# Splits ahead of the first norm's squares and sums on VectorE; the last output tile in two token parts, each with its own norm and stores

## The chip, the core and the metric

The kernel runs on one core of a Trainium2 chip. Its engines work side by side, each through a list of its own in order: TensorE (PE; its weight loads are shown as PEld), VectorE (DVE), ScalarE (ACT), GpSimd (POOL) and SyncE (SP); SyncE and ScalarE also issue the transfers. The metric is device time in microseconds (us), as a median of runs.

## What is computed

One step of a hybrid decoder of two layers: a gated delta-rule mixer (layer 0) and an RWKV-7 mixer (layer 1), each followed by a causal convolutional FFN, for a prompt of 512 tokens with 16 meta tokens ahead of it, and for 8 sequences of 4 new tokens. Everything is float32. Cut to what matters here:

```python
def rmsnorm(x, g):
    y = x * lax.rsqrt(jnp.mean(x * x, axis=-1, keepdims=True) + 1e-6)
    return y * g

def conv_ffn(h, buf, w_up, conv_w, w_down):
    up2 = h @ w_up                               # 1024 -> 2 * 2816
    gt, up = up2[..., :D_FF], up2[..., D_FF:]
    gc, new_buf = causal_dwconv(buf, gt, conv_w) # three taps
    return (silu(gc) * up) @ w_down, new_buf     # 2816 -> 1024

for i in range(2):
    x = x + mixer_i(rmsnorm(x, norm_mix[i]), ...)
    x = x + conv_ffn(rmsnorm(x, norm_ffn[i]), ...)
y = rmsnorm(x, norm_final)
```

The outputs are y for 544 tokens and the mixers' and convolutions' new states.

## The kernel before

The activations lie transposed: eight tiles (m = 0 to 7) of 128 features by 560 tokens (528 of the prompt with the meta tokens, 32 of the samples); in the second FFN only the 544 tokens remain whose output is wanted. A matrix product is a sum of three products of TensorE: each float32 factor is split into hi (rounded to the type fp32r) and lo (the rest), and hi x hi, hi x lo and lo x hi are added up in PSUM (`dense_g`, line 115). A weight comes in pieces of up to eight tiles of 128 x 128: `load_piece` (lines 64 to 72) has ScalarE issue the transfer into raw, ScalarE makes hi, VectorE makes lo. raw, hi and lo have two buffers each, so a piece's hi has to wait until TensorE has used up the piece two before it. `E.plan` lists the pieces in their order; `fetch` loads one ahead.

A norm is not applied before the product that uses it. The squares of the eight x tiles are added up (class `Norm`, line 204: the first square into s, six more through sq, the eighth into sl), one-column matmuls with a column of ones sum them over the features (`sums`, line 231), VectorE works out the inverse root in eleven small instructions (`rsqrt`), matmuls spread it over the partitions (`spread`, line 244), and it is multiplied onto the product's result. x itself is only scaled by the norm's gain and split (`split_x`, lines 186 and 187: hi on ScalarE, lo on VectorE).

**The first inputs** (`first_input`). For each m: split, then `norm.add` with `spread=True`, so the squares alternate between ScalarE and VectorE; the six additions into s are GpSimd's (line 218). The first products are those of w_ab (32 columns) and of the first piece of w_in; both run over the eight x tiles as these become ready, and the norm's column sums follow them on TensorE.

**The last outputs** (`ffn` with layer 1, and the end of `body`). Each of the eight output tiles of the second FFN is a product over 22 tiles of h (pieces of 8, 8 and 6) in two halves of 272 tokens: 22 x 3 x 2 = 132 matmuls. VectorE adds the residual (xo, line 336), the sink squares it, adds the square and stores x times the gain in a tile that stays in SBUF (line 2022). After the eighth tile comes the final norm: sums, rsqrt, spread with two copies to SBUF (line 246), eight products y = x * s of 544 tokens (line 2053, two of them on GpSimd), and eight stores of 272 KB from a ring of three y tiles (line 2054).

The program is written as loops; a scheduler of the framework puts the instructions of each engine in order by a simulated timeline. So an edit at one place can also change the order elsewhere.

Of the kernel before, what the change touches and what calls it, by code (L numbers as in the profile page):

```python
# [8 lines left out]
F32 = mybir.dt.float32  # L9
# [3 lines left out]
ALU = mybir.AluOpType  # L13
# [47 lines left out]
    return E.pv[:, PV[name] + j:PV[name] + j + n]  # L61


def load_piece(E, src, kt, M, lo_eng, R=P):
    nc = E.nc
    raw = E.wp.tile([P, KD, P], F32, tag="raw", name="raw", bufs=2)
    hi = E.wp.tile([P, KD, P], F32R, tag="hi", name="hi")
    lo = E.wp.tile([P, KD, P], F32R, tag="lo", name="lo")
    nc.scalar.dma_start(out=raw[:R, :kt, :M], in_=src)
    nc.scalar.activation(hi[:R, :kt, :M], raw[:R, :kt, :M], AF.Copy)  # L70
    lo_eng.tensor_tensor(lo[:R, :kt, :M], raw[:R, :kt, :M], hi[:R, :kt, :M].bitcast(F32), op=ALU.subtract)  # L71
    return hi, lo
# [13 lines left out]
def plan(E, src, kts, M=P, eng=None, R=P):  # L86

    k = 0
    for kt in kts:
        E.plan.append((src[:, k:k + kt, :], kt, M, eng or E.nc.vector, R))  # L90
        k += kt
# [50 lines left out]
def dense(E, kts, xs, split, M=P, room=None, n=T):  # L142
    g = dense_g(E, kts, xs, split, M, None, room, n)
    while True:
        try:
            next(g)
        except StopIteration as e:
            return e.value
# [21 lines left out]
def big_pair(E, name, rings):  # L170

    return [big(E, F32R, name, r) for r in rings]


def tiles(pair, n=KD):
    return [(pair[0][:, k], pair[1][:, k]) for k in range(n)]
# [13 lines left out]
class Norm:  # L190
# [10 lines left out]
            self.E.nc.gpsimd.memset(t[:, self.w:], 1.0)  # L201
        return t

    def add(self, x, tmp, spread=False):
        E, nc = self.E, self.E.nc
        if self.n == 0:
            sq = self.acc
        elif self.n < KD - 1:
            sq = tmp.tile([P, T], F32, tag="sq", name="sq")
        else:  # L210
            sq = self.last = self.room("sl")
        sq = sq[:, :self.w]
        if spread and self.n % 2:
            nc.vector.tensor_tensor(sq, x, x, op=ALU.mult)
        else:
            nc.scalar.activation(sq, x, AF.Square)  # L216
        if 0 < self.n < KD - 1:
            nc.gpsimd.tensor_tensor(self.acc[:, :self.w], self.acc[:, :self.w], sq, op=ALU.add)  # L218
        self.n += 1

    def scale(self, bank):
# [25 lines left out]
        return self.acc  # L247


def first_input(E):  # L250

    nc = E.nc
    with ExitStack() as st:
        tp = E.pool("x0", 2, stack=st)
        norm, pair = Norm(E), big_pair(E, "x", (0, 0))
        xs = [tp.tile([P, T], F32, tag="x", name="x", bufs=KD) for _ in range(KD)]
        for m in range(KD):
            nc.sync.dma_start(out=xs[m], in_=E.I["xT"][m])
            if m == 3:
                nc.sync.dma_start(out=E.cm, in_=E.I["cm"])  # L260
        for m in range(KD):
            split_x(E, xs[m], pvec(E, "norm_mix0", m), pair[0][:, m], pair[1][:, m])
            norm.add(xs[m], tp, True)
    return pair, norm


def plan_ffn(E, layer):
    for j in range(KF):
        plan(E, E.I["w_up"][layer, j], [KD])
        plan(E, E.I["w_up"][layer, KF + j], [KD])  # L270
    for m in range(KD):
        plan(E, E.I["w_down"][layer, m], [8, 8, 6])


def ffn(E, layer, xs, norm, ring, x_dram, sink):

    nc, I, O = E.nc, E.I, E.O

# [7 lines left out]
    with ExitStack() as st:  # L286
# [3 lines left out]
        nc.sync.dma_start(out=state, in_=I["ffn_state"][layer])  # L290
        news = ar.tile([P, KF, 18], F32, tag="fnew", name="fnew")
        bank = bank_of(E.pool(f"ffnp{layer}", 3, PSUM, stack=st))
        hb = big_pair(E, "hb", ring)
        hs = []
        for j in range(KF):
# [36 lines left out]
        for m in range(KD):  # L332
            xo = tp.tile([P, n_main], F32, tag="xo", name="xo")
            nc.sync.dma_start(out=xo, in_=x_dram[m][:, :n_main])
            ps = dense(E, [8, 8, 6], hs, hw, n=n_main)
            nc.vector.tensor_tensor(two(xo), ps[:, :, :hw], two(xo), op=ALU.add)
            sink(m, xo, tp)
# [101 lines left out]
def bank_of(pg):  # L439
    def bank(shape):  # L440
        t = pg.tile([P, 512], F32, tag="pg", name="pg")
        n = int(np.prod(shape))
        v = t[:, :n]
        if len(shape) == 2:
            v = v.rearrange("p (a b) -> p a b", a=shape[0])
        elif len(shape) == 3:
            v = v.rearrange("p (a b c) -> p a b c", a=shape[0], b=shape[1])
        return v
    return bank
# [1548 lines left out]
def body(nc, tc, I, O):  # L1998
    with ExitStack() as st:
# [43 lines left out]
        gdn(E, p0, n0, I["xT"], then(big_pair, (0, 1), "norm_ffn0", res[0]))  # L2043
        ffn(E, 0, tiles(later["x"]), later["n"], (0, 1), res[0], then(big_pair, (0, 1), "norm_mix1", res[1]))
        rwkv(E, later["x"], later["n"], res[1], then(big_pair, (0, 0), "norm_ffn1", res[2]))
        ffn(E, 1, tiles(later["x"]), later["n"], (1, 1), res[2], then(big, 0, "norm_final", None))
        x = later["x"]
        s = later["n"].scale(bank_of(E.pool("pf", 3, PSUM)))
        tp = E.pool("fin", 3)
        for m in range(KD):  # L2050
            y = tp.tile([P, TL], F32, tag="y", name="y")
            eng = nc.gpsimd if m % 3 == 2 else nc.vector
            eng.tensor_tensor(y, x[:, m, :TL], s[:, :TL], op=ALU.mult)
            nc.sync.dma_start(out=O["y"][m], in_=y)


# [24 lines left out]
```

## Time and profile before

| | us |
|---|---|
| median of 3 runs | 1897.88 |
| fastest and slowest of them | 1892.95, 1904.3 |
| the profiled execution | 1895.85 |
| its span, from the first to the last instruction | 1894.0 |
| TensorE busy in the span | 1791.6 |
| VectorE, ScalarE, GpSimd busy | 1153.9, 731.3, 369.9 |
| mean granted clock of TensorE, as a share of full speed | 0.952 |

How to read the profile: times are us from the span's start. A row of the timeline has start, duration, engine, line, operation, out<-in, the count of merged instructions, and in brackets how long the engine had been idle and what ended that. In the chain of waits, a row has start, duration and what the end of the program was waiting for at that time. In the table of groups a row has busy time, mean ns of one, and the idle time before it with its releasers.

### The profile page before, as it was taken

The numbers are of one execution on the slowest core, as the hardware profiler recorded it, in microseconds if no ns is written. First come the engines' busy times: TensorE is split into PE (matmuls) and PEld (weight loads), VectorE is DVE, ScalarE is ACT, GpSimd is POOL, SyncE is SP. The second block draws the span as 40 slices with busy tenths as digits, with TensorE's granted clock in tenths as the row PEclk, the third lists the DMA queues.
The fourth block names the chain that finished last, engine by engine and source line by source line (L and its number), as shares of the span: only waits on it lengthen the run. The fifth ranks groups of instructions, "written<-read, shape, count | busy, mean of one in ns | idle before, by whom it ended". The sixth has DMA issues, their size and how long they took to land.

```text
span 1894.0 us, 36463 instructions
## 1 busy us (share of the span) xinstructions
PE 1791.6 (95%) x14675; PEld 1711.5 (90%) x14675; DVE 1153.9 (61%) x2321; ACT 731.3 (39%) x1479; POOL 369.9 (20%) x616
## 2 busy tenths in 40 slices
PE   7999999999999999998998999799997999999996
PEld 6889998789999999998788998688787999999996
DVE  6688973874555553336788986775666455554223
ACT  4776434442322232221882246444323222222221
POOL 3442402621222221114011010020001111111011
PEclk9999998999999999999897999797898899999998
DMA  4233232333222223434212244332255222222331
GB/s 132 77 88 99 65 97 100 145 117 131 83 85 90 81 88 100 122 118 120 72 63 67 83 115 127 93 97 84 76 152 156 86 88 90 90 90 91 101 109 67
DMA packets 128674, 186.23 MB, mean 98 GB/s; under 512 B 63753, under 2 KB 76041, under 8 KB 128505
## 3 DMA queue, kind: packets, MB, share of 16 engines
q10 hardware_dynamic: 34448, 111.63, 18.5%
q1 hardware_dynamic: 94056, 72.27, 13.2%
q8 instruction: 116, 1.90, 0.4%
q14 instruction: 54, 0.43, 0.1%
HBM read 151.63 MB, written 32.22 MB: 97 GB/s over the span
## 4 chain that ended last, share of the span: by engine, by line
PE 79%; DVE 10%; ACT 3%; DMA 2%; issue 1%; SPq 0%; POOL 0%; ACTq 0%; DVEq 0%
PE pd L115 58%; PE pd L138 3%; PE pg L1372 1%; PE pg L1674 1%; PE pg L1774 1%; PE pg L1651 1%; PE pg L1665 1%; PE pg L1647 1%; PE pg L1656 1%; DMA xo<-x 1%; DVE lo L71 1%; PE pg L835 1%; PE pg L627 1%; PE pg L1793 1%; PE pg L1466 0%
## 5 line engine op out<-in xcount | busy, mean ns | idle before, releaser
L115 PE MATMUL pd<-x,hi 128*128 128x280 f32 (+7 forms) x4768 | 838.1, 297 | 25.7 <-ACT hi L70 10.0
L115 PEld LDWEIGHTS pd<-x,hi 128*128 128x128 f32 (+1 forms) x4768 | 695.6, 192 | 33.1 <-ACT hi L70 10.2
L115 PE MATMUL pd<-x,lo 128*128 128x296 f32 (+5 forms) x2384 | 514.7, 297 | 5.9 <-DVE lo L71 5.9
L70 ACT ACTIVATE hi<-raw 128x1024 fp32r<-128x1024 f32 (+3 forms) x218 | 220.0, 1009 | 510.8 <-PE pd L115 476.6
L115 PEld LDWEIGHTS pd<-x,lo 128*128 128x128 f32 (+1 forms) x2384 | 383.5, 192 | 9.6 <-DVE lo L71 6.9
L71 DVE TENSOR_TENSOR lo<-raw,hi 128x1024 fp32r<-128x1024 f32 (+3 forms) x218 | 253.5, 1163 | 219.8 <-ACT hi L70 213.0
L218 POOL TENSOR_TENSOR s<-s,sq 128x560 f32<-128x560 f32 (+2 forms) x30 | 50.6, 1685 | 309.1 <-ACT sq L216 278.8
L304 DVE TENSOR_TENSOR gp<-pd,s 128x528 f32<-128x528 f32 (+1 forms) x44 | 30.8, 701 | 106.9 <-PE pd L115 106.8
L115 PE MATMUL pd<-hl,hi 128*128 128x280 f32 (+1 forms) x448 | 93.4, 290 | 0.0
L115 PE MATMUL pd<-hh,hi 128*128 128x280 f32 (+1 forms) x448 | 93.2, 289 | 0.0
L115 PE MATMUL pd<-hh,lo 128*128 128x280 f32 (+1 forms) x448 | 93.1, 289 | 0.0
L115 PE MATMUL pd<-hb,hi 128*128 128x280 f32 (+1 forms) x512 | 85.8, 289 | 0.0
L316 ACT ACTIVATE gs<-cv 128x528 f32<-128x528 f32 (+1 forms) x44 | 28.1, 639 | 147.3 <-DVE cv L314 147.3
L115 PEld LDWEIGHTS pd<-hb,hi 128*128 128x128 f32 x512 | 72.8, 188 | 0.0
L115 PEld LDWEIGHTS pd<-hh,lo 128*128 128x128 f32 x448 | 70.8, 188 | 0.0
L115 PEld LDWEIGHTS pd<-hl,hi 128*128 128x128 f32 x448 | 70.5, 188 | 0.0
L115 PEld LDWEIGHTS pd<-hh,hi 128*128 128x128 f32 x448 | 70.5, 188 | 0.0
L319 POOL TENSOR_TENSOR gs<-gs,s 128x560 f32<-128x560 f32 (+1 forms) x44 | 60.8, 1381 | 37.9 <-ACT gs L317 37.9
L322 DVE TENSOR_TENSOR h<-pd,gs 128x560 f32<-128x560 f32 (+1 forms) x44 | 32.1, 730 | 57.0 <-POOL gs L319 57.0
L308 POOL COPY fnew<-gp 128x2 f32<-128x2 f32 x44 | 8.1, 185 | 294.1 <-DVE gp L304 294.1
L138 PE MATMUL pd<-os,hi 128*128 128x280 f32 x256 | 53.0, 303 | 2.5 <-ACT os L183 1.9
L115 PE MATMUL pd<-hb,lo 128*128 128x280 f32 (+1 forms) x256 | 53.3, 289 | 0.0
(547 smaller groups left out, 2959.6 us busy)
## 6 DMA issues: line engine op xcount, KB each, us to landing
raw<-w_up ACTq DMA_DIRECT2D x88, 512.0 KB
raw<-w_in ACTq DMA_DIRECT2D x32, 512.0 KB
raw<-w_down ACTq DMA_DIRECT2D x32, 512.0 KB
raw<-w_down ACTq DMA_DIRECT2D x16, 384.0 KB
kbd<-kst SPq DMA_DIRECT2D x18, 256.0 KB
KB<-kbd SPq DMA_DIRECT2D x18, 256.0 KB
xd<-xo SPq DMA_DIRECT2D x16, 280.0 KB
raw<-gdn_out ACTq DMA_DIRECT2D x8, 512.0 KB
```

The lines of the kernel that those rows point to most:

```text
L70: nc.scalar.activation(hi[:R, :kt, :M], raw[:R, :kt, :M], AF.Copy)
L71: lo_eng.tensor_tensor(lo[:R, :kt, :M], raw[:R, :kt, :M], hi[:R, :kt, :M].bitcast(F32), op=ALU.subtract)
L115: nc.tensor.matmul(ps[b][:M, :c1 - c0] if isinstance(ps, list) else ps[:M, b, :c1 - c0], lhsT=w[:, kk, :M], rhs=x[:, c0:c1], start=(k == 0 ...
L138: nc.tensor.matmul(ps[:, b, :c1 - c0], lhsT=a, rhs=x[:, c0:c1], start=(k == i == 0), stop=(k == len(xs) - 1 and i == 2))
L218: nc.gpsimd.tensor_tensor(self.acc[:, :self.w], self.acc[:, :self.w], sq, op=ALU.add)
L304: nc.vector.tensor_tensor(two(gp[:, m0:]), pm, two(s[:, mo:mo + ml]), op=ALU.mult)
L316: nc.scalar.activation(gs[:, mo:mo + ml], cv[:, m0 - 2:], AF.Silu)
L319: nc.gpsimd.tensor_tensor(gs, gs, s[:, :n_main], op=ALU.mult)
L322: nc.vector.tensor_tensor(two(h), ps[:, :, :hw], two(gs), op=ALU.mult)
L627: nc.tensor.matmul(pa[:, c, :], lhsT=K[:, h, o:o + n], rhs=X[:, h, o:o + n], start=True, stop=True)
L835: nc.tensor.matmul(pt[:64], lhsT=kz[h % 2][:, b, :], rhs=S0s[h][:, b, :], start=(b == 0), stop=(b == 7))
L1372: nc.tensor.matmul(pa[hh][:, u], lhsT=KB[r, 4 * G + u, c], rhs=KR[r, 4 * G + u, c], start=True, stop=True)
```

## The change

Two edits, put into one version.

At the start, all eight splits are written ahead of the eight squares, and `norm.add` is told to use VectorE for its additions. At the end, the eighth output tile (m = 7) of the second FFN is made by a new `dense_parts`: it fetches the tile's three weight pieces, does all 66 matmuls of tokens 0 to 279, hands that part on, and then does the 66 of tokens 280 to 543. After each part a new `Norm.part` makes the norm of those tokens alone: it squares the part, sums with the column of ones, takes rsqrt of 70 x 4 values, and spreads them to PSUM. `ends` then multiplies the eight tiles' part by it, with VectorE reading the PSUM bank, and stores it: sixteen stores of 280 or 264 tokens from a ring of four y tiles. So that the three pieces can be held at once, the last of the tile gets hi and lo buffers of its own (`E.last_room`). GpSimd has no part in the last products any more.

```diff
--- before.py
+++ after.py
@@ -61,11 +61,10 @@
     return E.pv[:, PV[name] + j:PV[name] + j + n]
 
 
-def load_piece(E, src, kt, M, lo_eng, R=P):
+def load_piece(E, src, kt, M, lo_eng, R=P, room=None):
     nc = E.nc
     raw = E.wp.tile([P, KD, P], F32, tag="raw", name="raw", bufs=2)
-    hi = E.wp.tile([P, KD, P], F32R, tag="hi", name="hi")
-    lo = E.wp.tile([P, KD, P], F32R, tag="lo", name="lo")
+    hi, lo = [(room or E.wp).tile([P, kt if room else KD, P], F32R, tag=t, name=t) for t in ("hi", "lo")]
     nc.scalar.dma_start(out=raw[:R, :kt, :M], in_=src)
     nc.scalar.activation(hi[:R, :kt, :M], raw[:R, :kt, :M], AF.Copy)
     lo_eng.tensor_tensor(lo[:R, :kt, :M], raw[:R, :kt, :M], hi[:R, :kt, :M].bitcast(F32), op=ALU.subtract)
@@ -201,7 +200,7 @@
             self.E.nc.gpsimd.memset(t[:, self.w:], 1.0)
         return t
 
-    def add(self, x, tmp, spread=False):
+    def add(self, x, tmp, spread=False, eng=None):
         E, nc = self.E, self.E.nc
         if self.n == 0:
             sq = self.acc
@@ -215,7 +214,7 @@
         else:
             nc.scalar.activation(sq, x, AF.Square)
         if 0 < self.n < KD - 1:
-            nc.gpsimd.tensor_tensor(self.acc[:, :self.w], self.acc[:, :self.w], sq, op=ALU.add)
+            (eng or nc.gpsimd).tensor_tensor(self.acc[:, :self.w], self.acc[:, :self.w], sq, op=ALU.add)
         self.n += 1
 
     def scale(self, bank):
@@ -247,6 +246,25 @@
         return self.acc
 
 
+    def part(self, x, c, bank, tmp):
+
+        E, nc = self.E, self.E.nc
+        if c.start == 0:
+            self.last = self.room("sl")
+        nc.scalar.activation(self.last[:, c], x[:, c], AF.Square)
+        ps, po = bank([4]), bank([280])
+        for i, a in enumerate((self.acc, self.last)):
+            for j in range(4):
+                o = c.start + 70 * j
+                nc.tensor.matmul(ps[:70, j:j + 1], lhsT=a[:, o:o + 70], rhs=E.ones[:, 0:1], start=(i == 0 and j == 0), stop=(i == 1 and j == 3))
+        v, s5 = [tmp.tile([70, 4], F32, tag=t, name=t, bufs=2) for t in ("pv", "ps5")]
+        nc.vector.tensor_scalar(v, ps[:70, 0:4], 1.0 / 1024.0, 1e-6, op0=ALU.mult, op1=ALU.add)
+        rsqrt(E, tmp, s5, v, [70, 4], "pr")
+        for j in range(4):
+            nc.tensor.matmul(po[:, 70 * j:70 * j + 70], lhsT=s5[:, j:j + 1].to_broadcast([70, P]), rhs=E.ident[:70, :70], start=True, stop=True)
+        return po
+
+
 def first_input(E):
 
     nc = E.nc
@@ -260,7 +278,8 @@
                 nc.sync.dma_start(out=E.cm, in_=E.I["cm"])
         for m in range(KD):
             split_x(E, xs[m], pvec(E, "norm_mix0", m), pair[0][:, m], pair[1][:, m])
-            norm.add(xs[m], tp, True)
+        for m in range(KD):
+            norm.add(xs[m], tp, True, nc.vector)
     return pair, norm
 
 
@@ -269,10 +288,32 @@
         plan(E, E.I["w_up"][layer, j], [KD])
         plan(E, E.I["w_up"][layer, KF + j], [KD])
     for m in range(KD):
-        plan(E, E.I["w_down"][layer, m], [8, 8, 6])
-
-
-def ffn(E, layer, xs, norm, ring, x_dram, sink):
+        w = E.I["w_down"][layer, m]
+        if layer == 1 and m == KD - 1:
+
+            plan(E, w, [8, 8])
+            E.plan.append(lambda: [load_piece(E, w[:, 16:22, :], 6, P, E.nc.vector, room=E.last_room)])
+        else:
+            plan(E, w, [8, 8, 6])
+
+
+def dense_parts(E, kts, xs, cuts):
+
+    nc = E.nc
+    ps = E.pd.tile([P, 2, 512], F32, tag="pd", name="pd")
+    w = []
+    for kt in kts:
+        fetch(E)
+        hi, lo = E.ready.pop(0)
+        w += [(hi[:, k, :], lo[:, k, :]) for k in range(kt)]
+    for b, (c0, c1) in enumerate(zip(cuts, cuts[1:])):
+        for k, ((hi, lo), (xh, xl)) in enumerate(zip(w, xs)):
+            for i, (a, x) in enumerate(((hi, xh), (hi, xl), (lo, xh))):
+                nc.tensor.matmul(ps[:, b, :c1 - c0], lhsT=a, rhs=x[:, c0:c1], start=(k == i == 0), stop=(k == len(xs) - 1 and i == 2))
+        yield slice(c0, c1), ps[:, b, :c1 - c0]
+
+
+def ffn(E, layer, xs, norm, ring, x_dram, sink, ends=None):
 
     nc, I, O = E.nc, E.I, E.O
 
@@ -290,6 +331,8 @@
         nc.sync.dma_start(out=state, in_=I["ffn_state"][layer])
         news = ar.tile([P, KF, 18], F32, tag="fnew", name="fnew")
         bank = bank_of(E.pool(f"ffnp{layer}", 3, PSUM, stack=st))
+        if layer == 1:
+            E.last_room = E.pool("wl", 1, stack=st)
         hb = big_pair(E, "hb", ring)
         hs = []
         for j in range(KF):
@@ -332,6 +375,11 @@
         for m in range(KD):
             xo = tp.tile([P, n_main], F32, tag="xo", name="xo")
             nc.sync.dma_start(out=xo, in_=x_dram[m][:, :n_main])
+            if ends is not None and m == KD - 1:
+                for c, ps in dense_parts(E, [8, 8, 6], hs, (0, 280, n_main)):
+                    nc.vector.tensor_tensor(xo[:, c], ps, xo[:, c], op=ALU.add)
+                    ends(xo, c, bank, ar)
+                continue
             ps = dense(E, [8, 8, 6], hs, hw, n=n_main)
             nc.vector.tensor_tensor(two(xo), ps[:, :, :hw], two(xo), op=ALU.add)
             sink(m, xo, tp)
@@ -2043,15 +2091,17 @@
         gdn(E, p0, n0, I["xT"], then(big_pair, (0, 1), "norm_ffn0", res[0]))
         ffn(E, 0, tiles(later["x"]), later["n"], (0, 1), res[0], then(big_pair, (0, 1), "norm_mix1", res[1]))
         rwkv(E, later["x"], later["n"], res[1], then(big_pair, (0, 0), "norm_ffn1", res[2]))
-        ffn(E, 1, tiles(later["x"]), later["n"], (1, 1), res[2], then(big, 0, "norm_final", None))
-        x = later["x"]
-        s = later["n"].scale(bank_of(E.pool("pf", 3, PSUM)))
-        tp = E.pool("fin", 3)
-        for m in range(KD):
-            y = tp.tile([P, TL], F32, tag="y", name="y")
-            eng = nc.gpsimd if m % 3 == 2 else nc.vector
-            eng.tensor_tensor(y, x[:, m, :TL], s[:, :TL], op=ALU.mult)
-            nc.sync.dma_start(out=O["y"][m], in_=y)
+        def ends(x, c, bank, tmp):
+
+            t, n = later["x"], c.stop - c.start
+            po = later["n"].part(x, c, bank, tmp)
+            nc.scalar.activation(t[:, KD - 1, c], x[:, c], AF.Copy, scale=pvec(E, "norm_final", KD - 1))
+            for m in range(KD):
+                y = tmp.tile([P, 280], F32, tag="y", name="y", bufs=4)[:, :n]
+                nc.vector.tensor_tensor(y, t[:, m, c], po[:, :n], op=ALU.mult)
+                nc.sync.dma_start(out=O["y"][m][:, c], in_=y)
+
+        ffn(E, 1, tiles(later["x"]), later["n"], (1, 1), res[2], then(big, 0, "norm_final", None), ends)
 
 
 def kernel(**inputs):
```

What the scheduler makes of it. On VectorE at the start, before (x<-x is a split, sq<-x and sl<-x a square, s<-s,sq an addition, lo<-raw a weight's lo):

```order
L214 TENSOR_TENSOR sq<-x 128x560
L187 SCALAR_TENSOR_TENSOR x<-x,pv 128x560 x2
L71 TENSOR_TENSOR lo<-raw,hi 128x8x32
L187 SCALAR_TENSOR_TENSOR x<-x,pv 128x560
L214 TENSOR_TENSOR sq<-x 128x560
L71 TENSOR_TENSOR lo<-raw,hi 128x1024
L187 SCALAR_TENSOR_TENSOR x<-x,pv 128x560 x2
L214 TENSOR_TENSOR sq<-x 128x560
L187 SCALAR_TENSOR_TENSOR x<-x,pv 128x560
L214 TENSOR_TENSOR sl<-x 128x560
L187 SCALAR_TENSOR_TENSOR x<-x,pv 128x560 x2
```

The same place on VectorE now, up to the last square but one:

```order
L213 TENSOR_TENSOR sq<-x 128x560
L186 SCALAR_TENSOR_TENSOR x<-x,pv 128x560
L217 TENSOR_TENSOR s<-s,sq 128x560
L186 SCALAR_TENSOR_TENSOR x<-x,pv 128x560
L70 TENSOR_TENSOR lo<-raw,hi 128x8x32
L186 SCALAR_TENSOR_TENSOR x<-x,pv 128x560
L217 TENSOR_TENSOR s<-s,sq 128x560
L213 TENSOR_TENSOR sq<-x 128x560
L70 TENSOR_TENSOR lo<-raw,hi 128x1024
L186 SCALAR_TENSOR_TENSOR x<-x,pv 128x560
L217 TENSOR_TENSOR s<-s,sq 128x560
L186 SCALAR_TENSOR_TENSOR x<-x,pv 128x560 x2
```

The splits do not move ahead of the squares as the text of the program has them: the order of splits and squares stays nearly what it was, and the six additions (three of them in these rows) stand between them on VectorE. After these rows follow the square of the eighth tile, a split, an addition, a square, the eighth split and the last two additions.

On TensorE at the end of the program, before (hb, hh and hl are h, pg<-cm,s and sl the column sums, the last row the spread):

```order
L115 MATMUL pd<-hl,hi 128x272 x2
L115 MATMUL pd<-hh,lo 128x272 x2
L231 MATMUL pg<-cm,s 70x1 x8
L231 MATMUL pg<-cm,sl 70x1 x8
L244 MATMUL pg<-cm,ns 128x70 x8
```

The same place now (ps_19955 is the first part's inverse root, ps_20077 the second's):

```order
L312 MATMUL pd<-hh,lo 128x264
L312 MATMUL pd<-hh,hi 128x264
L264 MATMUL pg<-cm,ps_19955 128x70 x4
L312 MATMUL pd<-hl,hi 128x264
L312 MATMUL pd<-hh,lo 128x264
L259 MATMUL pg<-cm,s 70x1 x4
L259 MATMUL pg<-cm,sl 70x1 x4
L264 MATMUL pg<-cm,ps_20077 128x70 x4
```

The first part's spread stands two matmuls ahead of the end of the second part. Its column sums stand further up, those of s between the two parts and those of sl behind the first sixteen matmuls or so of the second.

On VectorE at the end, before (ns is the inverse root, y the output):

```order
L354 TENSOR_TENSOR rst<-rsi,nv 70x8
L355 SCALAR_TENSOR_TENSOR rst<-rst,rsi 70x8
L356 SCALAR_TENSOR_TENSOR ns<-rst,rsi 70x8
L246 COPY s<-pg 128x280 x2
L2053 TENSOR_TENSOR y<-x,s 128x544 x6
```

The same place now, from the end of the first part's rsqrt to the start of the second's (xo is the residual of the second part, pv its mean square):

```order
L403 SCALAR_TENSOR_TENSOR rst<-rst,rsi 70x4
L404 SCALAR_TENSOR_TENSOR ps_19955<-rst,rsi 70x4
L2101 TENSOR_TENSOR y<-x,pg 128x280 x4
L380 TENSOR_TENSOR xo<-pd,xo 128x264
L2101 TENSOR_TENSOR y<-x,pg 128x280 x4
L261 TENSOR_SCALAR pv<-pg 70x4
L399 TENSOR_SCALAR rsi<-pv 70x4
```

Four of the first part's products stand ahead of the second part's residual and four behind it, ahead of the second part's norm.

Elsewhere the order changes at a few places of the gated delta mixer, and more in the first stretch of the RWKV mixer (in the trace of before, about 900 to 975 us): there ScalarE's sequence of exponentials and sigmoids is dealt out differently, with two activation-table loads fewer (32 in the program, before 34), and the weights' lo steps and some of TensorE's small products stand elsewhere between their neighbours.

## The prediction

> **What bounds the kernel now.** I read the page first (busy shares, then the shares of the chain that ended last), then the stretch that each half of the change touches: the timeline of the first 48 us by engine, and the chain from 1800 us on.
>
> ```profile
> span 1894.0 us, 36463 instructions
> PE 1791.6 (95%) x14675; PEld 1711.5 (90%) x14675; DVE 1153.9 (61%) x2321; ACT 731.3 (39%) x1479; POOL 369.9 (20%) x616
> PE 79%; DVE 10%; ACT 3%; DMA 2%; issue 1%; SPq 0%; POOL 0%; ACTq 0%; DVEq 0%
> ```
>
> TensorE is busy for 95% of the span and holds 79% of the chain. So a change off TensorE can pay only where TensorE stands still: at the start, where it waits for the split inputs, and behind its last matmul, where it has nothing left. These are the change's two places. First VectorE at the start (start, duration, instruction, its wait):
>
> ```profile
> 5.75 0.74 DVE L214 TENSOR_TENSOR sq<-x 128x560 f32<-128x560 f32 x1 [0.71 <-DMA x<-xT]
> 6.41 2.62 DVE L187 SCALAR_TENSOR_TENSOR x<-x,pv 128x560 fp32r<-128x560 f32 x2
> 9.03 0.42 DVE L71 TENSOR_TENSOR lo<-raw,hi 128x256 fp32r<-128x256 f32 x1
> 9.68 0.80 DVE L187 SCALAR_TENSOR_TENSOR x<-x,pv 128x560 fp32r<-128x560 f32 x1 [0.23 <-ACT x L186]
> 10.40 1.94 DVE L214 TENSOR_TENSOR sq<-x 128x560 f32<-128x560 f32 x1
> 12.26 1.21 DVE L71 TENSOR_TENSOR lo<-raw,hi 128x1024 fp32r<-128x1024 f32 x1
> 13.40 3.79 DVE L187 SCALAR_TENSOR_TENSOR x<-x,pv 128x560 fp32r<-128x560 f32 x2
> ...
> 20.33 2.63 DVE L187 SCALAR_TENSOR_TENSOR x<-x,pv 128x560 fp32r<-128x560 f32 x2
> 24.59 1.22 DVE L71 TENSOR_TENSOR lo<-raw,hi 128x1024 fp32r<-128x1024 f32 x1 [1.63 <-ACT hi L70]
> ```
>
> The same split takes 0.80 at 9.68 and 1.9 in the pair at 13.40; a square takes 0.74 at 5.75 and 1.94 at 10.40. The last split ends at 22.96. What runs beside the slow ones, who waits, and TensorE's own dates:
>
> ```profile
> L218 POOL TENSOR_TENSOR s<-s,sq 128x560 f32<-128x560 f32 x6 | 10.9, 1824 | 8.8 <-ACT x L186 5.3 <-ACT sq L216 1.9 <-DVE sq L214 1.4
> PEld pd L115 <- DVE x L187: 3.6, 4, 1.2
> 9.05 1.14 PE L115 MATMUL pd<-x,hi 128*32 128x280 f32 x4 [9.05 <-ACT hi L70]
> 26.15 1.12 PE L231 MATMUL pg<-cm,s 128*70 128x1 f32 x16
> 29.00:32.50 3.50, 3.50 (x18) 0.52 0.41 150
> 32.50:36.00 3.50, 3.50 (x30) 0.99 0.00 0
> 465.74 397.22 PE pd L115 x3072
> ```
>
> Six GpSimd additions of 1.82 lie beside the slow VectorE instructions, and TensorE's weight loads wait 3.6 us for splits. (The window rows give TensorE's busy time with its instructions, the granted clock, the DMA share and GB/s: 18 matmuls against 30 in equal stretches.)
>
> **The start, worked out.** Pitches, from one start to the next: split 0.72 (9.68 to 10.40), square 0.66 (5.75 to 6.41), lo of a full weight 1.14 (12.26 to 13.40). An addition on VectorE isn't shown; as a two-input instruction of the square's shape I take 0.66. Below, it can hardly be under 0.66; above, if one took GpSimd's 1.82, four of them would add 4.6 us and eat the whole term. I take the square's, since shape, type and engine are the same.
>
> With the new list the third split still starts at 9.68 (lo at 9.03 waits for its weight). From there to the eighth split's start stand five splits (3.60), three additions (1.98), three squares (1.98) and one lo (1.14): 8.7 us. The eighth starts at 18.4 and ends at 19.2, for 22.96 now: 3.8 earlier. Two additions follow, to 20.6.
>
> TensorE has 96 matmuls ahead of the column sums, at 397.22/3072 = 0.129 each. It starts at 9.05 as before and runs 24 (3.1) until it needs the full weight's lo at about 12.9; the other 72 take 9.3 and end at 22.2, with every split ready ahead of its matmuls. The column sums (now at 26.15) start at about 22.3; sums finished at 20.6 cover their input. They are two groups like the 1.12 one, 2.2 us, so the next weight's lo has to be there at 24.5. It ends 2.9 behind the last split now (22.96 to 25.81), because its hi buffer is freed by the matmuls of that split; those will end at about 21.4, and 2.9 later is 24.3: no new wait. VectorE's rsqrt steps stand behind that lo as before. **Gain 3.8 us**, and it carries, since TensorE is the bound behind it and the weights' transfers are released by its own matmuls.
>
> The half-rate stretch from 29.0 costs 12 matmuls of 0.117, 1.4 us, and follows those 2.2 us of one-column sums. Those sums stay, so I leave it in the sum; if it goes, 1.4 more, and if a second comes, 1.4 less. The Trainium skill (TensorE: Matmul & The Clock Gate, Part 1) says the clock is set by free-running windows of 3.4 us that a kernel's start does not reset; the length agrees with the row, and by that rule the stretch would be luck.
>
> **The end, worked out.** The chain behind the last matmul, then prices from elsewhere:
>
> ```profile
> 1799.97 73.26 PE pd L115 x582
> ...
> 1878.12 3.70 PE pg L244 x16
> ...
> 1884.84 2.05 DMA out_y<-y
> ...
> 1889.90 0.72 DVE y L2053
> ```
>
> ```profile
> 1873.25 0.72 DVE L336 TENSOR_TENSOR xo<-pd,xo 128x544 f32<-128x544 f32 x1 [9.01 <-PE pd L115]
> 1874.01 0.66 ACT L216 ACTIVATE sl<-xo 128x544 f32<-128x544 f32 x1 [10.76 <-DVE xo L336]
> 1875.93 0.16 DVE L235 TENSOR_SCALAR nv<-pg 70x8 f32<-70x8 f32 x1 [1.95 <-PE pg L231]
> 1880.20 0.45 DVE L246 COPY s<-pg 128x280 f32<-128x280 f32 x1 [2.14 <-PE pg L244]
> 462.53 1.74 PE pg L244 x16
> 409.95 37.05 PE pd L138 x286
> 1044.64 1.63 DMA LI<-L
> 1037.30 3.43 DMA LI<-L
> ```
>
> From 1873.23 to the span's end at 1894.0 are 20.8 us. After the change:
>
> - TensorE's last tile. The same 132 matmuls, now with one weight after another into one half. The similar line 138 runs at 37.05/286 = 0.130 per 280 columns, line 115 at 0.129, so the new order is free. New within it: the first part's sums (16 of the one-column instructions at 1.12/16, 1.1 us) and its spread (half of 1.74 on a running TensorE, 0.9). The last matmul ends at 1875.2, 2.0 later. The third weight piece has its own buffers and is ready early.
> - VectorE. The first part's spread stands two matmuls ahead of the end, so its eight products come at the end too: four ahead of the second part's xo, four behind. At 0.45 each (the 280-column row), 0.39 apart, four end at 1876.5; xo 0.43 and the square 0.38 (a little over half of the 0.72 and 0.66 above) and sums 0.6 bring the second part's sums to 1878.0. But the second four products wait on the ring of four y tiles: a product that ends at 1875.4, stored in 2.05, lets the fifth start at 1877.45, the eighth at 1878.6, done at 1879.1. The second norm is queued behind it: 1.1 us of new wait.
> - From there: rsqrt chain 2.2 (1875.93 to 1878.12) to 1881.3; spread on a rested TensorE 2.08 (1878.12 to 1880.20) to 1883.4; the copies of s fall away, since the products read PSUM. Eight products of 264 columns, four by four through the ring: four at 0.37, then a wait of 2.5 from the first's start, four more; the last ends at 1887.4. Now the last ends at 1890.6, 3.4 ahead of the span's end. So the end comes at 1890.8: **gain 3.2 us.**
>
> Of a half-size store the trace has none. Nearest: 2.05 for 272 KB here; 1.63 and 3.43 for 32 KB elsewhere. Each 0.4 less or 1.4 more counts three times (both rings and the last store): 4.4 gain at the one end, a loss of about 1 at the other. I take 2.05, the row of this very place. The Trainium skill (DMA: Bandwidth & Descriptors, Anatomy of one DMA) gives about 2.0 us fixed per DMA plus bytes over 436 GB/s, measured there for DMAs that GpSimd issues; that makes an estimated 2.3 for a half store and 2.6 for a full one. The full one measured 2.05 here, so the rule is too dear; by it the end's gain would be 2.4.
>
> **Between the two.** The scheduler also deals the RWKV mixer's first part differently; ScalarE has two table loads fewer there.
>
> ```profile
> 965.30 0.47 ACT L1227 ACTIVATE sg<-pg,pv 128x256 f32<-128x256 f32 x1
> 965.79 1.28 ACT L1254 ACT_TABLE_LOAD   x1
> 967.80 0.82 DVE L1266 SCALAR_TENSOR_TENSOR KR<-KR,pv 128x576 f32<-128x576 f32 x1 [1.89 <-ACT KR L1254]
> 965.97 0.83 PE L115 MATMUL pd<-x,lo 128*128 128x304 f32 x2 [2.77 <-DVE lo L71]
> ```
>
> The load at 965.79 and the one ahead of 965.30 go, as that piece of sg moves ahead of a KB step. This makes KB 0.5 later, and with it the lo that TensorE waits for at 965.97; VectorE's idle 1.89 goes. Between -0.6 and +2.6 (both loads); I count nothing.
>
> **Sum.** 3.8 + 3.2 + 0 = 7.0. The profiled execution took 1895.85 (1.85 around its span): 1888.9. The median of the runs shown is 1897.88, 2.0 above it: **1890.9.** A measurement of this kernel tells about 0.5%, 9.5 us, from no change, so this is a gain inside that bound.
>
> **Rivals.**
> 1. More comes out: the saved table loads (2.6) reach TensorE, and the half-rate stretch at the start goes (1.4): gain 11, 1886.9. For it: VectorE does wait for ScalarE there (1.89). Against: the loads stand behind the lo that TensorE waits for. 20%.
> 2. The end gives nothing: stores at 3.43 stretch both rings, the second norm waits 2.5 instead of 1.1, the end loses 1: gain 2.8, 1895.1. Against: no load runs beside these stores, as it did at 1037. 14%. That the parts hardly overlap, as the order has it, is in my sum already.
> 3. Slower: half-rate stretches. A shift of 4 us puts every later pause elsewhere.
>
> ```profile
> 1000.00:1050.00 50.00, 46.30 (x479) 0.81 0.27 63
> ```
>
> At a granted 0.81 about 19 of 50 us ran at half rate. One stretch costs 1.4; five more eat the gain, eight make it 4 slower, 1902. Nothing in the change adds pauses, so 8%, half of it beyond 0.5%.
>
> My forecast has 58%, from 4 to 10 us of gain. The range, 1885.5 to 1895.5, takes in gains from 12.4 to 2.4. Faster by over 0.5%: rival 1 and the top of the forecast, 26%; slower by over 0.5%, 4%; the rest 70%.
>
> **What would show it.** Right: splits of 0.8 throughout and the last ending near 19.2; column sums near 22.3; last matmul 2.0 later relative to the tile's start; a VectorE wait on stores ahead of the second norm; 15.6 us from the last matmul to the end. Wrong: additions over 1 us on VectorE, TensorE waiting for lo in the first 24 us, half stores over 3 us, or a gap that opens or closes between 40 and 1850 us by more than 2 us.

## The result, and the profile after

The changed kernel took 1886.45 us in the median of 20 runs (1882.79 to 1901.7), the kernel before 1900.09 in 20 (1890.15 to 1906.48). The ratio is 0.9936, with a 95% interval from 0.9921 to 0.9951: 12 us less. The prediction was 1890.9, a gain of 7. Its range holds the result; the result is the case to which it gave 26%, faster by over 0.5%.

The profiled execution of the changed kernel took 1896.1 us, nearly as long as that of the kernel before (1895.85), and longer than 18 of its other 19 runs. So the two profiles are compared stage by stage, not by their ends. First the page of the changed kernel:

```profile
span 1894.3 us, 36496 instructions
PE 1797.7 (95%) x14675; PEld 1716.2 (91%) x14675; DVE 1151.7 (61%) x2347; ACT 728.8 (38%) x1479; POOL 353.4 (19%) x608
PE 77%; DVE 12%; ACT 3%; DMA 2%; issue 1%; SPq 0%; POOL 0%; ACTq 0%; DVEq 0%
```

**The start.** VectorE in the changed kernel (start, duration, instruction, its wait):

```profile
6.23 0.79 DVE L186 SCALAR_TENSOR_TENSOR x<-x,pv 128x560 fp32r<-128x560 f32 x1
6.94 0.73 DVE L217 TENSOR_TENSOR s<-s,sq 128x560 f32<-128x560 f32 x1
...
14.00 1.51 DVE L186 SCALAR_TENSOR_TENSOR x<-x,pv 128x560 fp32r<-128x560 f32 x2
15.43 0.73 DVE L213 TENSOR_TENSOR sl<-x 128x560 f32<-128x560 f32 x1
...
18.10 0.80 DVE L186 SCALAR_TENSOR_TENSOR x<-x,pv 128x560 fp32r<-128x560 f32 x1
18.81 1.58 DVE L217 TENSOR_TENSOR s<-s,sq 128x560 f32<-128x560 f32 x2
```

Every split takes 0.80, every addition 0.73, every square 0.73, and the last split ends at 18.90 (22.96 before). TensorE:

```profile
8.85 1.14 PE L114 MATMUL pd<-x,hi 128*32 128x280 f32 x4 [8.85 <-ACT hi L69]
...
13.05 1.56 PE L114 MATMUL pd<-x,hi 128*128 128x296 f32 x6
14.44 0.42 PE L114 MATMUL pd<-x,lo 128*128 128x296 f32 x2
...
23.68 1.12 PE L230 MATMUL pg<-cm,s 128*70 128x1 f32 x16
```

No wait stands between 8.85 and 23.68: TensorE no longer waits for splits. In the kernel before it waited three times:

```profile
17.25 0.44 PE L115 MATMUL pd<-x,hi 128*32 128x280 f32 x2 [0.75 <-DVE x L187]
...
21.17 0.44 PE L115 MATMUL pd<-x,hi 128*32 128x280 f32 x2 [0.82 <-DVE x L187]
...
23.02 0.45 PE L115 MATMUL pd<-x,hi 128*32 128x280 f32 x2 [0.89 <-DVE x L187]
```

But the column sums come at 23.68, not at the 22.3 of the prediction (26.15 before).

**The end.** The chain that ended last, and VectorE's products with their waits:

```profile
1877.99 0.86 PE pg L264 x8
...
1879.35 1.79 DMA out_y<-y
...
1885.30 1.96 PE pg L264 x8
...
1887.74 1.74 DMA out_y<-y
```

```profile
1868.84 0.45 DVE L380 TENSOR_TENSOR xo<-pd,xo 128x280 f32<-128x280 f32 x1 [5.55 <-PE pd L312]
...
1878.88 1.51 DVE L2101 TENSOR_TENSOR y<-x,pg 128x280 f32<-128x280 f32 x4 [3.98 <-PE pg L264]
1880.31 0.43 DVE L380 TENSOR_TENSOR xo<-pd,xo 128x264 f32<-128x264 f32 x1
1881.24 1.91 DVE L2101 TENSOR_TENSOR y<-x,pg 128x280 f32<-128x280 f32 x4 [0.50 <-DMA out_y<-y]
1883.07 0.15 DVE L261 TENSOR_SCALAR pv<-pg 70x4 f32<-70x4 f32 x1
...
1889.58 1.94 DVE L2101 TENSOR_TENSOR y<-x,pg 128x264 f32<-128x264 f32 x4 [0.84 <-DMA out_y<-y]
```

The second norm (1883.07) stands behind four products that wait on stores, as forecast. The last matmul ends near 1879.1, so 15.2 us to the span's end of 1894.3, where 15.6 was forecast and 20.8 stood before.

**Between the two.** TensorE's busy time with its instructions, the granted clock, the DMA share and GB/s, first of the kernel before, then of the changed one:

```profile
906.40:909.81 3.41, 2.50 (x14) 1.00 0.26 102
909.81:913.22 3.41, 3.13 (x12) 0.50 0.46 154
913.22:916.63 3.41, 3.41 (x17) 1.00 0.00 0
```

```profile
905.18:908.59 3.41, 1.82 (x10) 1.00 0.44 154
908.59:942.73 34.14, 34.14 (x103) 0.50 0.12 40
942.73:946.14 3.41, 3.41 (x22) 0.98 0.00 0
```

(A row has the window, its length, then these four.) At the same place of the RWKV mixer TensorE runs at half rate for one window of 3.41 us in the one profile and for ten on end in the other. For such 104 matmuls the kernel before takes 20 us:

```profile
915.00:925.00 10.00, 10.00 (x45) 1.00 0.08 29
925.00:935.00 10.00, 10.00 (x59) 1.00 0.15 54
```

So this profile lost some 14 us there, which most runs of the changed kernel cannot have lost. The two profiles account for about 6 us; 12 were measured. That is what the experiments ask about.

### The profile page after: what moved, and what is told of

Read it like the earlier page. It is cut to its first block, busy times and chain, and to the rows that moved or that the text cites. A ratio compares the mean times of both kernels' runs of the same rounds, so it can differ in the third digit from the quotient of the medians.

```text
span 1894.3 us, 36496 instructions
## 1 busy us (share of the span) xinstructions
PE 1797.7 (95%) x14675; PEld 1716.2 (91%) x14675; DVE 1151.7 (61%) x2347; ACT 728.8 (38%) x1479; POOL 353.4 (19%) x608
## 4 chain that ended last, share of the span: by engine, by line
PE 77%; DVE 12%; ACT 3%; DMA 2%; issue 1%; SPq 0%; POOL 0%; ACTq 0%; DVEq 0%
PE pd L114 56%; PE pd L137 3%; PE pg L1420 1%; DVE lo L70 1%; DMA xo<-x 1%; PE pg L1699 1%; DVE it L473 1%; PE pg L1722 1%; PE pd L312 1%; PE pg L1269 1%; PE pg L1713 1%; PE pg L1822 1%; PE pg L1695 1%; PE pg L883 1%; PE pg L1704 1%
## 5 line engine op out<-in xcount | busy, mean ns | idle before, releaser
L217 POOL TENSOR_TENSOR s<-s,sq 128x560 f32<-128x560 f32 (+2 forms) x24 | 39.9, 1662 | 299.1 <-ACT sq L215 273.1
L114 PE MATMUL pd<-hl,hi 128*128 128x280 f32 (+1 forms) x420 | 87.6, 290 | 0.0
L114 PE MATMUL pd<-hh,hi 128*128 128x280 f32 (+1 forms) x420 | 87.4, 289 | 0.0
L114 PE MATMUL pd<-hh,lo 128*128 128x280 f32 (+1 forms) x420 | 87.3, 289 | 0.0
L114 PE MATMUL pd<-hb,hi 128*128 128x280 f32 (+1 forms) x480 | 80.5, 290 | 0.0
L114 PEld LDWEIGHTS pd<-hb,hi 128*128 128x128 f32 x480 | 68.2, 188 | 0.0
L114 PEld LDWEIGHTS pd<-hh,lo 128*128 128x128 f32 x420 | 66.4, 188 | 0.0
L114 PEld LDWEIGHTS pd<-hh,hi 128*128 128x128 f32 x420 | 66.1, 188 | 0.0
L641 DVE SCALAR_TENSOR_TENSOR cv<-gp,pv,cv 128x584 f32<-128x584 f32 x48 | 42.2, 879 | 14.7 <-POOL cv L639 14.5
```

Source lines behind the costliest of these rows:

```text
L114: nc.tensor.matmul(ps[b][:M, :c1 - c0] if isinstance(ps, list) else ps[:M, b, :c1 - c0], lhsT=w[:, kk, :M], rhs=x[:, c0:c1], start=(k == 0 ...
L217: (eng or nc.gpsimd).tensor_tensor(self.acc[:, :self.w], self.acc[:, :self.w], sq, op=ALU.add)
L641: nc.vector.scalar_tensor_tensor(cv, gp[:, i:i + 584], cw[i], cv, op0=ALU.mult, op1=ALU.add)
```

## The experiments

Three theories of the missing 6 us: M, the new order in the mixer brings them; S or E, the start or the end is worth more than its trace shows; N, half-rate stretches fall differently in each execution and add noise to the mean. Each kernel was timed against the kernel before on the same chip, and each left a profile. The table has the ratio with its interval, and from the profile five columns in us: the dates of the first step of the first norm's inverse root and of the second's on VectorE, then three lengths: the RWKV mixer (from the third norm's such step to the fourth's), the last FFN from there to the seventh tile's residual, and from that to the end of the span.

| kernel | ratio (95%) | 1st norm | 2nd norm | mixer | to tile 7 | end |
|---|---|---|---|---|---|---|
| before | | 28.32 | 455.39 | 605.0 | 383.4 | 37.4 |
| before, as a change | 1.0005 (0.998 to 1.003) | 29.54 | 459.91 | 608.0 | 383.7 | 37.5 |
| the change | 0.9936 (0.9921 to 0.9951) | 26.10 | 454.92 | 609.9 | 383.8 | 34.0 |
| the change again | 0.9952 (0.9927 to 0.9977) | 26.14 | 452.87 | 611.8 | 380.8 | 33.9 |
| start alone | 0.9974 (0.9947 to 1.0002) | 23.88 | 454.63 | 616.0 | 383.6 | 37.1 |
| start, old mixer order | 0.9971 (0.9952 to 0.999) | 24.30 | 452.80 | 605.2 | 383.2 | 37.2 |
| mixer order alone | 0.9982 (0.996 to 1.0004) | 28.07 | 454.71 | 610.9 | 383.3 | 37.4 |
| end alone | 0.9953 (0.9933 to 0.9973) | 27.95 | 457.51 | 603.7 | 381.7 | 33.9 |
| end alone again | 0.9977 (0.9956 to 0.9998) | 28.13 | 456.87 | 610.6 | 380.8 | 33.9 |
| the change, old mixer order | 0.9949 (0.9929 to 0.9969) | 25.75 | 454.33 | 603.0 | 381.8 | 33.9 |
| ring of eight | 0.9957 (0.9931 to 0.9983) | 25.67 | 454.68 | 607.4 | 379.9 | 34.3 |
| ring of eight, products deferred | 0.9962 (0.9947 to 0.9976) | 25.04 | 455.94 | 604.5 | 383.4 | 32.6 |
| zeros ahead | 0.9969 (0.9944 to 0.9994) | 30.73 | 458.92 | 601.9 | 380.7 | 33.7 |
| zeros and deferred | 0.997 (0.9951 to 0.9989) | 31.84 | 460.16 | 603.7 | 383.3 | 32.6 |

**The start alone.** The new first inputs with the old end.

```diff
...
-            norm.add(xs[m], tp, True)
+        for m in range(KD):
+            norm.add(xs[m], tp, True, nc.vector)
```

> Only the start's half of the change, the old end; the scheduler gives it the changed kernel's order in the RWKV mixer as well. The changed kernel measured 12 us under the old one, where the two traces account for 2.0 us at 48 us and 3.6 us behind the last tile's start: some 6 us are looked for. Theory M (the new order in the mixer brings them): 8 us under the kernel before. Theory E (the end is worth more than its trace shows): 2 to 4 us under it, no more. Theory S (the start is worth more than the 2.0 that one execution shows, the 3.8 of the prediction or above): 4 us or more under it, with the column sums near 22.3 us.

0.9974, 5 us less, with an interval that reaches from 10 us to none. It does not choose between theories by itself. One half of this edit does nothing, as the engines' lists in the built programs show: with the splits written ahead and the additions left on GpSimd, the scheduler deals exactly the lists of the kernel before; with the additions alone moved, exactly those of this kernel. What acts is the additions' engine.

**The end alone.** The new end with the first inputs as before (the diff is against the change).

```diff
-        for m in range(KD):
-            norm.add(xs[m], tp, True, nc.vector)
+            norm.add(xs[m], tp, True)
```

> Only the end's half, the old start; every instruction ahead of the last output tile stands as in the kernel before, the mixer too. By the traces 3.6 us under the kernel before, by the prediction 3.2; theories M and S expect that. Theory E: 8 us or more. From the last tile's start to the end of the span 34.0 us as in the changed kernel, against 37.6.

0.9953, 8.9 us: theory E's number. Yet its trace shows the end at 33.9, as in the changed kernel, and 3.4 under the old one, so in that execution the rest is not in the end.

**The mixer's order alone.** Eight redundant ScalarE copies ahead of the first FFN.

```diff
                 split_x(E, x, pvec(E, gain, m), pair[0][:, m, :n], pair[1][:, m, :n])
+                for _ in range(8 if gain == "norm_ffn0" and m == 7 else 0):
+                    nc.scalar.activation(pair[0][:, m, :32], x[:, :32], AF.Copy, scale=pvec(E, gain, m))
```

> The kernel before with eight tiny ScalarE copies of 32 columns, which write again what is there already, at the last split ahead of the first FFN: they change the simulated timeline enough that the scheduler deals the RWKV mixer as in the changed kernel; start and end are the old ones. Theory M: 5 to 7 us under the kernel before. Theories S and E: no change, or up to 1.5 us slower by the eight copies (0.2 us each).

0.9982, 3.4 us less, with an interval from 7.6 us to less than nothing, which holds no change and theory M's 5 to 7 alike. The profiled mixer takes 610.9, longer than the 605.0 of the kernel before, so the profile gives theory M no support.

**The start in the old mixer order.** The first of the six additions stays on GpSimd (the diff is against the start alone).

```diff
-            norm.add(xs[m], tp, True, nc.vector)
+            norm.add(xs[m], tp, True, nc.vector if m in (2,3,4,5,6,) else None)
```

> The start's half with one of the six additions (the first) left on GpSimd: the mixer then keeps the order of the kernel before. Old end. Theory M: about 2 to 3 us under the kernel before, all of it ahead of 50 us. Theory S: 4 us or more, within 1 us of the run with all six additions on VectorE. Theory E: 2 to 3.

0.9971, 5.5 us, within 1 us of the start alone: the mixer's order is worth nothing that shows here, which speaks against theory M (its 2 to 3 us lie inside the interval, 1.9 to 9.1, too). Its VectorE list repeats what made the old start slow, with the one addition that GpSimd still has (6.29 to 8.07):

```profile
6.05 2.61 DVE L187 SCALAR_TENSOR_TENSOR x<-x,pv 128x560 fp32r<-128x560 f32 x2
...
13.03 1.51 DVE L187 SCALAR_TENSOR_TENSOR x<-x,pv 128x560 fp32r<-128x560 f32 x2
```

```profile
6.29 1.78 POOL L218 TENSOR_TENSOR s<-s,sq 128x560 f32<-128x560 f32 x1 [4.97 <-ACT x L186]
```

Two splits take 2.61 beside it and 1.51 without it. In the changed kernel, without a GpSimd addition, the splits at the same dates (6.23 and 7.59) take 0.79 and 0.80.

**The change again, the end alone again, and the kernel before measured as a change.** No edit.

> The changed kernel once more. Its trace accounts for 5.6 us (2.0 at the start, 3.6 at the end), the first measurement gave 12. If half-rate windows of TensorE in the mixer, which fall differently in each execution, are only noise on top (theory N), the gain here can lie anywhere from 4 to 13 us, and the profiled mixer need not take the 610 us of the first profile. If the change itself brings the rest (theory C), 10 us or more again.

> The end's half alone once more: all instructions ahead of the last tile stand as in the kernel before. Its first run gave 8.9 us (5.1 to 12.7) where the trace shows 3.6. Theory N: 3.6 lies in the interval this time, or the two together are nearer to it. Theory C: 8 us or more again, so that there is something in the end's half that neither trace shows.

> The kernel before as it is, measured as if it were a change: a ratio of 1 by any theory. How far it lies from 1, and whether the interval holds 1, says what such a measurement can tell of this kernel. Theory N: up to 0.3% from 1.

The change gave 9.1 us for 12.1, the end alone 4.4 for 8.9 (its interval from 0.4 to 8.3 holds the traced 3.4), and the kernel before 0.9 us more than itself. Theory E's 8 us did not come again, and the end took 33.9 in both traces. The two measurements of one kernel lie 3.0 and 4.5 us apart. The long stretch at half rate came again in the mixer order alone (ten windows from 909.90 on), and, with seven, in the second profile of the end alone, whose mixer stands in the old order:

```profile
910.00:920.00 10.00, 9.92 (x41) 0.82 0.22 81
920.00:930.00 10.00, 10.00 (x28) 0.50 0.00 1
930.00:940.00 10.00, 10.00 (x32) 0.50 0.17 54
940.00:950.00 10.00, 10.00 (x75) 0.98 0.16 52
```

and it did not come in the second profile of the changed kernel, which has the same instructions as the first:

```profile
910.00:920.00 10.00, 10.00 (x42) 0.90 0.07 29
920.00:930.00 10.00, 10.00 (x58) 1.00 0.17 55
930.00:940.00 10.00, 7.57 (x47) 0.79 0.04 11
```

So it belongs to the execution, not to the order. Among 35 runs of the kernel before, the granted clock and the time go together (correlation -0.93): 1888.39 at 0.956, 1907.37 at 0.946.

**The whole change in the old mixer order.**

```diff
-            norm.add(xs[m], tp, True, nc.vector)
+            norm.add(xs[m], tp, True, nc.vector if m > 1 else None)
```

> The whole change with one of the six additions (the first) left on GpSimd, which leaves the mixer in the order of the kernel before. In the six profiles so far the mixer took 603.7 to 605.2 us in the old order and 609.9 to 616.0 in the new. Theory O (the new order costs time on average): 3 us or more under the changed kernel of the same call. Theory N: within 2 us of it. The theory that the new order brings the missing 6 us: 4 us or more slower than the changed kernel.

0.9949 against 0.9952 for the change measured beside it: no difference, theory N's number. The mixer takes 605.9 on the mean of six profiles in the old order and 610.1 of six in the new, but with 603.0 to 610.6 and 604.5 to 616.0, and the timed runs do not show the 4 us. (The two kernels with zeros, below, whose VectorE list there is dealt a third way, took 601.9 and 603.7.)

No run decides between the theories alone, but the nine measurements so far can be taken together: 202 timed runs in three sessions, fitted with a level for each session and one amount each for the new start, the new end and the new mixer order. If the runs are independent, this estimate gives 4.5 us for the start (2.5 to 6.5), 5.5 for the end (3.7 to 7.3) and 0.6 for the order (from 2.6 gained to 1.5 lost). That excludes theory M's 5 to 7, and it leaves the start and the end together at 10.0 (7.8 to 12.1), above the 6 of the traces.

**A ring of eight y tiles.**

```diff
-                y = tmp.tile([P, 280], F32, tag="y", name="y", bufs=4)[:, :n]
+                y = tmp.tile([P, 280], F32, tag="y", name="y", bufs=8)[:, :n]
```

> The changed kernel with a ring of eight y tiles for four, so that no product waits for a store. The prediction put this wait at 1.1 us ahead of the second norm. In the trace of the changed kernel the fifth and sixth product start 1.9 us after the first pair ends. If the wait is what the second norm stands behind, the last matmul to the second norm's first step takes 4.6 us for 5.2, and the last eight products run on end (0.45 each), 0.6 less: 1.2 us from the tile's start to the end of the span. If the stores themselves are the bound (they queue for the same engines), no change.

The waits on stores went, and the end grew by 0.4, to 34.3:

```profile
1872.23 2.94 DVE L2101 TENSOR_TENSOR y<-x,pg 128x280 f32<-128x280 f32 x8 [4.00 <-PE pg L264]
1875.09 0.43 DVE L380 TENSOR_TENSOR xo<-pd,xo 128x264 f32<-128x264 f32 x1
1877.17 0.16 DVE L261 TENSOR_SCALAR pv<-pg 70x4 f32<-70x4 f32 x1 [1.66 <-PE pg L259]
```

With no wait between the products, the scheduler puts all eight ahead of the second part's residual. In the changed kernel the residual, the square and the column sums ran behind the wait; now they stand bare behind the products, from 1875.09 to 1877.17. Both accounts that were written down for this run were wrong: the wait was cover.

**Four products behind the second norm.**

```diff
...
+            def outs(ms, after=None):
+                for m in ms:
+                    y = tmp.tile([P, 280], F32, tag="y", name="y", bufs=8)[:, :n]
+                    if after is not None:
+                        nc.scalar.activation(y[:70, 0:4], after, AF.Copy)
+                    nc.vector.tensor_tensor(y, t[:, m, c], po[:, :n], op=ALU.mult)
+                    nc.sync.dma_start(out=O["y"][m][:, c], in_=y)
+            if c.start == 0:
+                outs(range(4))
+                later["rest"] = lambda s5: outs(range(4, KD), s5)
+            else:
+                later["rest"](later["n"].s5)
+                outs(range(KD))
```

> Eight y tiles, and four of the first part's products put behind the second norm: a four-column ScalarE copy of the second norm's result into their y tile, which the product overwrites, makes them wait for it. The second norm's steps then follow the residual at once, and the four products (1.8 us) run beside the spread on TensorE (2.0 us). By the chain of the changed kernel 2.5 us less from the last tile's start to the end (31.5 for 34.0). If the copies come late, or the spread is slowed by them, under 1.5.

```profile
1875.19 1.51 DVE L2106 TENSOR_TENSOR y<-x,pg 128x280 f32<-128x280 f32 x4 [3.99 <-PE pg L264]
1876.63 0.42 DVE L381 TENSOR_TENSOR xo<-pd,xo 128x264 f32<-128x264 f32 x1
1878.26 0.16 DVE L261 TENSOR_SCALAR pv<-pg 70x4 f32<-70x4 f32 x1 [1.21 <-PE pg L259]
...
1880.62 1.51 DVE L2106 TENSOR_TENSOR y<-x,pg 128x280 f32<-128x280 f32 x4 [0.27 <-ACT y L2105]
1882.49 2.81 DVE L2106 TENSOR_TENSOR y<-x,pg 128x264 f32<-128x264 f32 x8 [0.35 <-PE pg L264]
```

The four products run beside the second spread, and the end takes 32.6: 1.3 us less than the change, half of the 2.5 expected, because the square and the column sums (1.21 of wait) now stand ahead of the norm. Its time, 0.9962, cannot be told from that of the change.

**Zeros ahead of the first weight, alone and with the deferred products.**

```diff
...
+        z = wz.tile([P, 512], F32, tag="zero", name="zero")
+        nc.gpsimd.memset(z, 0.0)
+        zp = wp.tile([P, 512], F32, tag="zp", name="zp")
+        for i in range(6):
+            nc.tensor.matmul(zp[:128, :512], lhsT=z[:, :128], rhs=z, start=True, stop=True)
```

> The changed kernel with six matmuls of zeros (512 columns, nothing reads them) ahead of the first weight, while TensorE has nothing to do yet. In all traces TensorE ran at half rate from its first matmul near 9 us to 12.0 to 14.4; in the changed kernel that is 18 matmuls in 4.2 us for 2.3. If this is why the column sums came at 23.7 where the prediction had 22.3, they come at 22.0 to 22.5 here, and the stage ends 1.5 us earlier. If VectorE's splits set it (the last ends at 18.9), 23.0 or later still.

> The zeros at the start and the deferred products at the end in one kernel: the sum of the two, 4 us under the changed kernel if both hold, 14 under the kernel before. With the spread of half-rate windows in the mixer a measured gain of 10 to 18 us would agree.

Neither answers its question. With the zeros ahead, the scheduler put the eight transfers of x behind six others: SyncE issued them only from 8.51 on, the first square moved from 5.57 to 13.74, and TensorE stood still until 12.21 and started at half rate again (the trace has two records for each matmul of zeros):

```profile
1.31 7.17 PE L277 MATMUL zp<-zero 128*128 128x512 f32 x12 [1.31 <-POOL zero L274]
12.21 1.14 PE L114 MATMUL pd<-x,hi 128*32 128x280 f32 x4 [3.73 <-ACT x L185]
```

The ratios are 0.9969 and 0.997; a start with TensorE at full rate was not tried otherwise. The expectation was also wrong in its dates: with the start alone the stretch at half rate ended at 10.80, not at 12.0 or later. No version here beats the change by more than the measurement's uncertainty.

## Why the prediction was right or wrong

**The start, 3.8: mis-sized, 2.6 to 3.1.** VectorE's part held: splits of 0.80, additions of 0.73 where 0.66 from start to start was taken (their pitch is 0.65), the last split at 18.90 for 19.2, no wait for lo. The step that failed is TensorE's: "runs 24 (3.1) until it needs the full weight's lo". That priced its first matmuls at 0.129, though the row quoted above it has four in 1.14, at half rate. In the changed kernel the first 24 take 5.6 us, one every 0.233 us, up to 14.42, and 0.129 each behind it; the profile's granted clock reads 1.00 there all the same, since its record only begins at the end of this stretch. In the old start the slow matmuls were hidden behind the waits for splits: from the first matmul to the column sums it took 17.1 us whether they lasted 3.1 us (before) or 5.6 (the end alone), and in the latter the first of the three waits was gone. With the waits gone TensorE is the bound, and its start at half rate counts. The seven profiles of the new start, the zeros left out, show it by themselves. Each runs from its first matmul to the column sums without a wait, and the duration is 12.0 to 12.3 us plus half of the time at half rate: 13.84 with 3.2 at half rate (start alone), 13.60 with 2.7 (start in the old order), 14.83 with 5.6 (the change), 14.68 with 5.2 (again), and so in the other three, 13.9 to 15.0 with 3.5 to 5.8. The mean date of the first norm moved from 28.4 (five profiles of the old start) to 25.3 (seven of the new); at the second norm 2.6 of it are left, 456.9 to 454.3.

**The end, 3.2: right, 3.4.** From the seventh residual to the end it took 37.3 on the mean of five old ends and 33.9 to 34.0 in the five new ones with a ring of four and no zeros. The last matmul came 2.2 us later for 2.0; the second norm stood behind the ring and began 3.9 us after the last matmul, as in the sum. That the ring costs time did not come out: with eight tiles, in the order that the scheduler dealt for them, the norm began 4.7 after it. The half stores took 1.79 and 1.74 where 2.05 was taken. By the rule of the Trainium skill that was weighed there (DMA: Bandwidth & Descriptors, Anatomy of one DMA) they were an estimated 2.3: too dear, as for the full ones.

**The mixer, 0: held, within what can be seen.** The saved table loads of the first rival are not seen as time: the new order gave 3.4 us by itself with an interval from 7.6 to less than nothing, and none on top of the whole change; all runs together give 0.6, with the loads' 2.6 just at the edge. Its other half did not happen in the changed kernel's profile: the half-rate stretch of the start stayed, from 34.90 in place of 29.17.

**The half-rate stretches: the third rival had the mechanism, not the sign.** They move by more than the whole effect, 34 us on end at one place in one profile and at most 6.8 there in the next of the same program, and on both sides of the comparison. The prediction said that a gap of over 2 us that opens or closes between 40 and 1850 us would show it wrong. In the first profile one opened, since the mixer took 4.9 more. The timed runs have no stages; their 9 to 12 us against 6 traced rather point to one that closes.

**What stays open.** Start and end account for 6.0 us by the traces, close to the 7.0 of the sum. That the measured 12 lies inside the range is in part luck: about half of it comes from nothing in the sum. The intervals of both halves alone, except for the first run of the end, hold their traced amounts; of those of the whole change the first (9.3 to 15.0) lies above it, the second (4.4 to 13.8) holds it. A part lies at the entry of the last FFN, where instructions and order are unchanged: it took 383.2 to 383.7 up to the seventh residual in all five profiles with the old end, and 379.9 to 383.8, 381.8 on the mean, in nine with the new. The stretches at half rate make the difference: in all 14 profiles this stage is 378.2 to 379.9 us plus half of its time at half rate, 8.8 to 10.1 us in the five and 0 to 10.1 in the nine. They stand as in these rows of the kernel before and of the second profile of the change, of the 30 us around the fourth norm:

```profile
1464.00:1474.00 10.00, 10.00 (x84) 0.84 0.76 238
1474.00:1484.00 10.00, 8.14 (x58) 0.84 0.14 54
1484.00:1494.00 10.00, 9.57 (x56) 0.70 0.17 55
```

```profile
1465.60:1475.60 10.00, 10.00 (x86) 0.87 0.67 239
1475.60:1485.60 10.00, 7.71 (x63) 0.99 0.23 78
1485.60:1495.60 10.00, 10.00 (x70) 0.84 0.08 29
```

Whether the change makes them rarer there, or the profiles drew them so, the runs do not settle. The gain is 6 us whose places can be shown, and some 3 to 6 more whose places cannot.

## What to carry to other kernels

When a wait is removed, price what ran in its shadow again: here TensorE's start at half rate, and behind the y ring the residual and the sums, cost nothing until the wait in front of them was gone. Where a program's own spread is wider than an edit's worth, read the edit from the lengths of its stages in several profiles, and measure the kernel before against itself. An edit in the written order may do nothing, and one at the start may deal work anew a thousand instructions later: compare the engines' lists before pricing it.

## What the runs showed of the hardware

Behind the first matmuls, TensorE's half-rate stretches came in multiples of 3.41 us in every profile, but for the one that the program's end cuts off. A stretch of ten windows ran with TensorE busy for all of its 34.14 us, and so did one of ten (mixer order alone) and one of seven (end alone) elsewhere, while the kernel before ran the same matmuls at full rate. The Trainium skill (TensorE: Matmul & The Clock Gate, Part 1) has full speed come after at least one busy window of about 3.4 us; in these rows up to ten busy ones did not bring it. Matmuls with weights on 64 partitions stand among the others in the long stretches, and full speed came back 4.6, 4.6 and 3.4 us after the last of them had ended; that they are the cause wasn't tried.
